# A decoder layer's first FFN group: gate and up blocks in one pass instead of two

## The chip, the cores and the metric

The kernel runs on one core of a Trainium2 chip. The metric is the device time of one execution in microseconds, from the host's point of view the time of the one launch; the profiled span, from the first to the last instruction of the program, is a little shorter. TensorE multiplies, ACT (ScalarE) and DVE (VectorE) work on the operands and results, SP (SyncE) and ACT issue the transfers from memory.

## The reference

A decoder layer on x of 256 rows and 2048 columns, float32: a half-weighted SwiGLU FFN, then a mixing stage (causal pooling, forgetting attention, memory cross-attention, gated and merged), then a second half FFN. The FFN is

```
def swiglu_half_ffn(x, norm_g, w_gate_up, w_down):
    h = rmsnorm(x, norm_g)
    gate, up = jnp.split(h @ w_gate_up, 2, axis=-1)
    return 0.5 * ((jax.nn.silu(gate) * up) @ w_down)
```

with w_gate_up of 2048 x 11264 (5632 gate columns, then 5632 up columns) and w_down of 5632 x 2048. This case is about the first 512 columns of gate and of up in the first FFN, the first thing that the kernel computes.

## The kernel before

**Products.** Every float32 operand is split in two parts, a high one that ACT writes (a copy in fp32r) and a low one that DVE writes (operand minus high). A product of 128 rows of weights by 512 columns is three matmuls: high by high, and the two mixed ones (add_product, lines 240 to 244; mm_group has its own loop, line 352). With 256 rows of x there are two row tiles t, so a k-tile (128 rows of weights) by a block (512 columns) takes six matmuls. A block has 16 k-tiles. Cutting weights into high and low is called a cut here; its tiles are wh and wl, five buffers each, 1024 columns wide.

**x.** The rows of x stay in four tiles xc of 512 columns each. `prepare(c, jj)` makes one page of the left side (tile names x, lines 200, 189, 190): four transposes on TensorE into a bank, then for each of two k-tiles a high part on ACT and a low part on DVE, both scaled by the norm's gains (`cols0`, made from a small load, a transpose and a copy, line 125). The row statistics are taken later (`row_sums`, eight squares on ACT, line 364; `row_rstd`, a chain of small steps on DVE from line 368 to 179) and are needed only by the gates, `gated`, lines 453 and 455. `row_sums` is pinned on ACT behind the ACT instruction that was traced just before it.

**Groups.** The FFN's 11 groups c each take 512 gate columns and 512 up columns. Groups 1 to 10 use `pair_group`: eight units of two k-tiles, each loaded as one raw tile (three buffers of 1 MB) with both blocks. For a unit listed in `seven`, the 2 x 2 blocks (two k-tiles, two blocks, two row tiles) are multiplied with seven block products instead of eight, that is 21 matmuls instead of 24. That needs a form page of x for the unit, made by `form_page` and kept in `forms`; which units are so treated is read at the call:

```
        seven = list(forms) if seven is None else seven
```

Form pages are made for the k-tile pairs 0, 1 and 2. The products of such a unit read the tiles hah, hal, hbh, hbl. A group with such units holds eight PSUM banks, one without holds four; there are eight in all. Group 0 does not use pair_group but two passes of `mm_group`: first the gate block over all 16 k-tiles, then the up block. In the first pass its loads are of 1, 1, 1, 1, 2, 2, 4 and 4 k-tiles, and the loads of x are placed between them by `before`.

**Order.** A planner orders each engine's instructions by the order in which they are traced and by its own times; `keep_in_program_order` pins an instruction behind the one traced before it on its engine. Work beside the products stands in the queue `side`; each `tick()` takes one entry from it. mm_group ticks after each cut; pair_group ticks after each block of a unit, for units that lie after the last unit with seven products, or for all when there is none. Before, the queue at the start holds a pause, `prepare(0, 1)`, a pause, the six other prepares, row_sums, three form pages, `small_loads`, three pauses and `small_cols`. `small_loads` issues eleven small loads on ACT's queue (tile rows); having no inputs, they may be issued early.

Of the kernel before, what the change touches and what calls it, by code (L numbers as in the profile page):

```python
# [16 lines left out]
P = 128  # L17
# [16 lines left out]
def hybrid_layer(  # L34
# [68 lines left out]
    def load_x(c0, n):  # L103
        tc.keep_in_program_order(
            nc.sync.dma_start(out=xc[c0 // 512][:, :, c0 % 512 : c0 % 512 + n], in_=xv[:, :, c0 : c0 + n])
        )
# [138 lines left out]
                ps, sides[part], wt[i][:, col : col + 512], start=start and q == 0, stop=stop and q == 2  # L245
            )

    def pair_group(w, c0, c1, lhs, forms, order, seven=None, hook=None, early=False):

        seven = list(forms) if seven is None else seven
        at = [i for i, u in enumerate(order) if u in seven]
        acc, terms = {}, {}

        def into(key, last):
            if key not in acc:
                acc[key] = bank("mm")  # L260
                return acc[key], True, last
            return acc[key], False, last

        for i, u in enumerate(order):
            end = i == len(order) - 1
            if hook:
                hook(i, u)
            raw = wp.tile([P, 2, 2, 512], F32, tag="raw", name="raw")
            for n, cc in enumerate((c0, c1)):
                nc.sync.dma_start(  # L270
                    out=raw[:, n, :, :],
                    in_=w[2 * u * P : (2 * u + 2) * P, cc : cc + 512].rearrange("(k p) c -> p k c", p=P),
                )
            if u not in seven:
                for n in range(2):
                    wt = parts(1024)
                    cut(wt, raw[:, n, :, :].rearrange("p k c -> p (k c)"))
                    for t in range(T):
                        for kk in range(2):
                            ps, start, stop = into((t, n), end and kk == 1)  # L280
                            add_product(ps, [lhs(2 * u + kk, q, t) for q in range(2)], wt, kk * 512, start, stop)
                    if not at or i > at[-1] or 1 < i < at[0] or (early and i == 0):
                        tick()
                continue
            last = i == at[-1]
            s = raw.rearrange("p n k c -> p (n k) c")
            plain = parts(1024)
            cut(plain, s[:, 0:2, :].rearrange("p s c -> p (s c)"))
            ta, tb = page([2, 512], F32, "ta"), page([2, 512], F32, "tb")
            nc.vector.tensor_tensor(ta, s[:, 3:4, :].to_broadcast([P, 2, 512]), s[:, 1:3, :], ALU.add)  # L290
            ha = (page([1024], F32R, "hah"), page([1024], F32R, "hal"))
            cut(ha, ta.rearrange("p s c -> p (s c)"))
            plain2 = parts(512)
            cut(plain2, s[:, 2, :])
            nc.vector.tensor_tensor(tb[:, 0, :], ta[:, 0, :], s[:, 2, :], ALU.add)
            nc.vector.tensor_tensor(tb[:, 1, :], tb[:, 0, :], s[:, 0, :], ALU.add)  # L296
            hb = (page([1024], F32R, "hbh"), page([1024], F32R, "hbl"))
            cut(hb, tb.rearrange("p s c -> p (s c)"))
            fm = lambda m: [forms[u][:, q, m, :] for q in range(2)]
            xq = lambda kk, t: [lhs(2 * u + kk, q, t) for q in range(2)]  # L300
            for key, sides, wt, col in (
                ("p1", xq(1, 0), plain, 512),
                ((0, 0), xq(0, 0), plain, 0),
                ("p5", fm(0), ha, 0),
                ("p7", fm(2), ha, 512),
                ((0, 1), fm(3), plain2, 0),
                ("p6", fm(1), hb, 0),
                ((1, 0), xq(0, 1), hb, 512),
            ):
                ps, start, stop = into(key, last if isinstance(key, str) else end)  # L310
                add_product(ps, sides, wt, col, start, stop)
            if last:
                a, u3, u4, v = (temp([512], n) for n in ("ua", "u3", "u4", "uv"))
                nc.scalar.activation(a, acc["p1"], AF.Copy)
                nc.vector.tensor_tensor(u3, acc["p6"], a, ALU.add)
                nc.vector.tensor_tensor(u4, acc["p5"], u3, ALU.subtract)
                nc.vector.tensor_tensor(u3, acc["p7"], u3, ALU.add)
                nc.vector.tensor_tensor(v, acc["p5"], u3, ALU.subtract)
                terms = {(0, 0): a, (1, 0): u3, (0, 1): u4, (1, 1): v}
        return acc, terms  # L320

    def mm_group(w, c0, kt, lhs, cols=((0, 512),), before=None):

        ncol = sum(n for _, n in cols)
        per, half = 2048 // ncol, 1024 // ncol
        ps = [[bank("mm") for _ in cols] for _ in range(T)]
        cuts = [0, 1, 2, 3, 4, 6, *range(8, kt + 1, per)] if before else [*range(0, kt, per), kt]
        for k0, k1 in zip(cuts, cuts[1:]):
            nk = k1 - k0
            if k0 % per == 0:  # L330
                whole = wp.tile([P, per, ncol], F32, tag="raw", name="raw")
            raw = whole[:, k0 % per : k0 % per + nk, :]
            load = nc.sync.dma_start(
                out=raw,
                in_=w[k0 * P : (k0 + nk) * P, c0 : c0 + ncol].rearrange("(k p) c -> p k c", p=P),
            )
            if before:
                tc.keep_in_program_order(load)
            if before:
                before(k0)  # L340
            for h0 in range(0, nk, half):
                nh = min(half, nk - h0)
                wh, wl = (b.rearrange("p (k c) -> p k c", c=ncol) for b in parts(half * ncol))
                rv, hv, lv = raw[:, h0 : h0 + nh, :], wh[:, :nh, :], wl[:, :nh, :]
                nc.scalar.activation(hv, rv, AF.Copy)  # L345
                nc.vector.tensor_tensor(lv, rv, hv.bitcast(F32), ALU.subtract)  # L346
                for t in range(T):
                    for kk in range(nh):
                        k = k0 + h0 + kk
                        for i, (o, n) in enumerate(cols):  # L350
                            for q, (part, wt) in enumerate(((0, wh), (0, wl), (1, wh))):
                                nc.tensor.matmul(  # L352
                                    ps[t][i][:, :n],
                                    lhs(k, part, t),
                                    wt[:, kk, o : o + n],
                                    start=k == 0 and q == 0,
                                    stop=k == kt - 1 and q == 2,
                                )
                tick()
        return ps  # L360
# [51 lines left out]
    def ffn(lx, forms, rs, wgu, wd, stream, cb, before=None):  # L412
# [34 lines left out]
        def gated(c, gate, up):  # L447
            hd = []
            for t in range(T):
                s = gate[t]  # L450
                if c == 0:
                    s = temp([512], "sg")
                nc.scalar.activation(s, gate[t], AF.Silu, scale=rs[0][:, t : t + 1])
                h = temp([512], "hd") if c == 0 else up[t]
                nc.vector.scalar_tensor_tensor(h, up[t], rh[:, t : t + 1], s, ALU.mult, ALU.mult)
                hd.append(h)
            return hd

        pa = mm_group(wgu, 0, KD, lx, before=before)
        nc.vector.tensor_scalar(rh, rs[0], 0.5, None, ALU.mult)  # L460
        pb = mm_group(wgu, FF, KD, lx)
        hd = gated(0, [pa[t][0] for t in range(T)], [pb[t][0] for t in range(T)])
        side.extend(put(0, hd))
        for c in range(1, NFC):
            if c == NFC - 1:
# [54 lines left out]
    def prepare(c, jj):  # L520
        to_lhs_part(tiles0, jj, lambda t: xc[c][:, t, :], G_FFN1[:, 4 * c : 4 * c + 4], "x0")

    def before(k0):

        if k0 == 0:
            prepare(0, 0)
        elif k0 == 1:
            load_x(256, 256)
        elif k0 == 3:
            load_x(512, 512)  # L530
        elif k0 == 6:
            load_x(1024, 512)
        elif k0 == 8:
            load_x(1536, 512)

    def row_sums(cs):
        for c in cs:
            for t in range(T):
                tc.keep_in_program_order(sumsq(ss0, t, c, xc[c][:, t, :]))

    side.extend(pause + [lambda: prepare(0, 1)] + pause)
    for c in range(1, 4):
        side.append(lambda c=c: prepare(c, 0))
        side.append(lambda c=c: prepare(c, 1))
    side.append(lambda: row_sums(range(4)) or rs0.append(row_rstd(ss0, "x0")))
    forms0 = {}
    side.extend(form_steps(forms0, tiles0))
    side.append(small_loads)
    side.extend(pause * 3 + [small_cols])
    s0 = Stream([xv[:, :, c * 512 : (c + 1) * 512] for c in range(4)])  # L550
    cb, x1, rs, s1 = residual(s0, G_MIX, "x1")
# [419 lines left out]
```

## Time and profile before

| | us |
|---|---|
| time, median of 3 runs (2128.15 to 2128.83) | 2128.67 |
| time of the profiled execution | 2128.03 |
| its span | 2126.3 |

TensorE's busy time is 99% of the span, DVE's 82%, ACT's 56%; the granted clock of TensorE is 1.00 throughout. A busy time counts a matmul from its start to its modelled end, and neighbours overlap; distances between starts tell more.

### The profile page before, as it was taken

Reading aid. Unit: us, or ns where it says so; the run is one execution under the profiler, and the core shown is the slowest. Engines: PE = TensorE matmul, PEld = TensorE weight load, DVE = VectorE, ACT = ScalarE, POOL = GpSimd, SP = SyncE. Lnnn points to the kernel's source line nnn. Section 1 sums busy time; section 2 is a strip of 40 time slices with the busy share of each in tenths; the row PEclk is TensorE's granted clock in tenths of the full one; section 3 lists DMA queues with packets and bytes.
Section 4 is the critical chain, followed back from the end, with each engine's and each line's share of the span. In section 5 each row is a group of like instructions: output and inputs, shape, how many; then the busy total and the mean of one; then the engine's idle time right before and its main releaser. Section 6 shows DMA issues by size and latency. Waiting matters only on the chain.

```text
span 2126.3 us, 26105 instructions
## 1 busy us (share of the span) xinstructions
PE 2114.2 (99%) x9683; PEld 1744.7 (82%) x9683; DVE 1739.4 (82%) x2221; ACT 1186.1 (56%) x1488; POOL 3.5 (0%) x24
## 2 busy tenths in 40 slices
PE   9999999999999999999999999999999999999999
PEld 7888888888888888887788888878888888888887
DVE  7898899889858788657669878898899889989675
ACT  6555555556545565555655555565555555556453
POOL 0000000000000000000000000000000000000000
PEclk9999999999999999999999999999999999999999
DMA  7666666666866654754456656575666666677764
GB/s 260 206 213 212 207 210 216 211 230 223 274 211 205 225 204 149 250 165 157 139 178 217 198 189 211 195 250 199 214 217 207 209 208 218 208 235 245 258 193 148
DMA packets 221508, 444.67 MB, mean 209 GB/s; under 512 B 12654, under 2 KB 13764, under 8 KB 221380
## 3 DMA queue, kind: packets, MB, share of 16 engines
q1 hardware_dynamic: 221088, 442.96, 62.7%
q8 instruction: 76, 1.25, 0.2%
q14 instruction: 52, 0.43, 0.1%
q10 hardware_dynamic: 292, 0.05, 0.0%
HBM read 426.16 MB, written 16.79 MB: 208 GB/s over the span
## 4 chain that ended last, share of the span: by engine, by line
PE 97%; DVE 1%; DMA 1%; ACT 0%; issue 0%; SPq 0%; ACTq 0%; DVEq 0%
PE mm L244 74%; PE mm L352 20%; PE hid L428 1%; DMA raw<-in_ffn_w_gate_up_dram 1%; DVE wl L346 0%; PE x L200 0%; DVE xr L389 0%; PE fpt L851 0%; PE fav L861 0%; PE mg L200 0%; PE flg L823 0%; PE mlg L729 0%; PE mav L756 0%; PE flg L821 0%; ACT wh L345 0%
## 5 line engine op out<-in xcount | busy, mean ns | idle before, releaser
L238 ACT ACTIVATE wh<-raw 128x1024 fp32r<-128x1024 f32 x608 | 599.7, 988 | 634.6 <-PE mm L244 362.5
L239 DVE TENSOR_TENSOR wl<-raw,wh 128x1024 fp32r<-128x1024 f32 x608 | 682.4, 1132 | 204.6 <-ACT wh L238 203.8
L244 PE MATMUL mm<-wh,x 128*128 128x512 f32 x2300 | 713.5, 391 | 0.0
L244 PEld LDWEIGHTS mm<-wh,x 128*128 128x128 f32 x2300 | 428.7, 188 | 87.3
L244 PE MATMUL mm<-wl,x 128*128 128x512 f32 x1150 | 446.7, 390 | 0.0
L244 PE MATMUL mm<-wh,hid 128*128 128x512 f32 x1168 | 357.7, 390 | 0.0
L352 PE MATMUL mm<-wh,x 128*128 128x512 f32 (+1 forms) x960 | 291.7, 382 | 2.9 <-ACT x L189 2.8
L346 DVE TENSOR_TENSOR wl<-raw,wh 128x1024 fp32r<-128x1024 f32 (+2 forms) x170 | 196.8, 1161 | 95.8 <-ACT wh L345 94.9
L345 ACT ACTIVATE wh<-raw 128x1024 fp32r<-128x1024 f32 (+2 forms) x170 | 170.5, 1009 | 169.7 <-PE mm L352 97.3
L244 PEld LDWEIGHTS mm<-wh,hid 128*128 128x128 f32 x1168 | 218.8, 188 | 45.1
L244 PEld LDWEIGHTS mm<-wl,x 128*128 128x128 f32 x1150 | 215.9, 188 | 45.3
L244 PE MATMUL mm<-wl,hid 128*128 128x512 f32 x584 | 222.4, 389 | 0.0
L352 PEld LDWEIGHTS mm<-wh,x 128*128 128x128 f32 x960 | 175.6, 188 | 38.6 <-ACT x L189 4.2
L352 PE MATMUL mm<-wl,x 128*128 128x512 f32 (+1 forms) x480 | 181.4, 379 | 0.2 <-DVE wl L346 0.2
L290 DVE TENSOR_TENSOR ta<-raw 128x1024 f32<-128x1024 f32 x101 | 123.1, 1219 | 12.0 <-DMA raw<-in_ffn_w_gate_up_dram 6.4
L244 PEld LDWEIGHTS mm<-wl,hid 128*128 128x128 f32 x584 | 109.6, 188 | 22.8
L239 DVE TENSOR_TENSOR hbl<-tb,hbh 128x1024 fp32r<-128x1024 f32 x101 | 123.2, 1220 | 2.5 <-ACT hbh L238 2.3
L239 DVE TENSOR_TENSOR hal<-ta,hah 128x1024 fp32r<-128x1024 f32 x101 | 123.2, 1220 | 1.4 <-ACT hah L238 1.4
L238 ACT ACTIVATE hbh<-tb 128x1024 fp32r<-128x1024 f32 x101 | 106.3, 1053 | 30.1 <-DVE tb L296 30.0
L238 ACT ACTIVATE hah<-ta 128x1024 fp32r<-128x1024 f32 x101 | 106.3, 1052 | 27.5 <-DVE ta L290 27.1
L244 PE MATMUL mm<-hah,form 128*128 128x512 f32 x404 | 121.5, 389 | 0.0
L352 PEld LDWEIGHTS mm<-wl,x 128*128 128x128 f32 x480 | 90.1, 188 | 16.3 <-DVE wl L346 0.6
(318 smaller groups left out, 2198.2 us busy)
## 6 DMA issues: line engine op xcount, KB each, us to landing
raw<-in_ffn_w_gate_up_dram SPq DMA_DIRECT2D x322, 512.0 KB, 4.5
raw<-in_ffn_w_down_dram SPq DMA_DIRECT2D x176, 512.0 KB, 5.1
raw<-in_w_in_dram SPq DMA_DIRECT2D x80, 512.0 KB, 5.1
raw<-in_w_in_dram SPq DMA_DIRECT2D x36, 1024.0 KB, 5.0
raw<-in_w_out_dram SPq DMA_DIRECT2D x32, 512.0 KB, 5.1
raw<-in_ffn_w_gate_up_dram SPq DMA_DIRECT2D x14, 1024.0 KB, 5.6
hd<-hf SPq DMA_DIRECT2D x20, 512.0 KB, 5.1
hg<-hd SPq DMA_DIRECT2D x20, 512.0 KB, 8.5
```

Source lines behind the costliest of these rows:

```text
L238: nc.scalar.activation(dst[0], src, AF.Copy)
L239: nc.vector.tensor_tensor(dst[1], src, dst[0].bitcast(F32), ALU.subtract)
L244: nc.tensor.matmul(ps, sides[part], wt[i][:, col : col + 512], start=start and q == 0, stop=stop and q == 2)
L290: nc.vector.tensor_tensor(ta, s[:, 3:4, :].to_broadcast([P, 2, 512]), s[:, 1:3, :], ALU.add)
L345: nc.scalar.activation(hv, rv, AF.Copy)
L346: nc.vector.tensor_tensor(lv, rv, hv.bitcast(F32), ALU.subtract)
L352: nc.tensor.matmul(ps[t][i][:, :n], lhs(k, part, t), wt[:, kk, o : o + n], start=k == 0 and q == 0, stop=k == kt - 1 and q == 2,)
L428: nc.tensor.transpose(ps[:, j, t * P : (t + 1) * P], hd[t][:, k * P : (k + 1) * P], ident)
```

## The change

Group 0 of the first FFN (the call with `before`) is now one pair_group over units 0 to 7 with both blocks, with no seven-product units, with `hook=before` and `pieces=2`. In a group with pieces every load on SP is pinned to the traced order. The first two units are loaded in four pieces, one for each k-tile and block, and cut piece by piece, 512 columns at a time; the others are loaded as two halves of 512 KB. `before` is now called with the unit's place: it loads x 256 to 511 and then 512 to 1023 ahead of unit 1, x 1024 to 1535 ahead of unit 3 and 1536 to 2047 ahead of unit 5, and it makes the pages of x for the following products. The queue now begins with `small_loads`, followed by 13 pauses, row_sums, the form pages, three pauses and small_cols.

```diff
-    def pair_group(w, c0, c1, lhs, forms, order, seven=None, hook=None, early=False):
+    def pair_group(w, c0, c1, lhs, forms, order, seven=None, hook=None, early=False, pieces=0):
...
-            for n, cc in enumerate((c0, c1)):
-                nc.sync.dma_start(
-                    out=raw[:, n, :, :],
-                    in_=w[2 * u * P : (2 * u + 2) * P, cc : cc + 512].rearrange("(k p) c -> p k c", p=P),
-                )
+            step = 1 if i < pieces else 2
+            for k in range(0, 2, step):
+                for n, cc in enumerate((c0, c1)):
+                    one = nc.sync.dma_start(
+                        out=raw[:, n, k : k + step, :],
+                        in_=w[(2 * u + k) * P : (2 * u + k + step) * P, cc : cc + 512].rearrange(
+                            "(k p) c -> p k c", p=P
+                        ),
+                    )
+                    if pieces:
+                        tc.keep_in_program_order(one)
+            if i < pieces:
+                for kk in range(2):
+                    for n in range(2):
+                        wt = parts(512)
+                        cut(wt, raw[:, n, kk, :])
+                        for t in range(T):
+                            ps, start, stop = into((t, n), False)
+                            add_product(ps, [lhs(2 * u + kk, q, t) for q in range(2)], wt, 0, start, stop)
+                    tick()
+                continue
...
-        pa = mm_group(wgu, 0, KD, lx, before=before)
-        nc.vector.tensor_scalar(rh, rs[0], 0.5, None, ALU.mult)
-        pb = mm_group(wgu, FF, KD, lx)
-        hd = gated(0, [pa[t][0] for t in range(T)], [pb[t][0] for t in range(T)])
+        if before:
+            ps, _ = pair_group(wgu, 0, FF, lx, {}, range(8), hook=before, pieces=2)
+            nc.vector.tensor_scalar(rh, rs[0], 0.5, None, ALU.mult)
+            up = [ps[t, 1] for t in range(T)]
+            hd = gated(0, [ps[t, 0] for t in range(T)], up)
+        else:
+            pa = mm_group(wgu, 0, KD, lx)
...
-    def before(k0):
+    def before(i, u):
-        if k0 == 0:
+        if i == 0:
             prepare(0, 0)
-        elif k0 == 1:
+        if i == 1:
             load_x(256, 256)
-        elif k0 == 3:
+            prepare(0, 1)
             load_x(512, 512)
-        elif k0 == 6:
+        if i == 2:
+            prepare(1, 0)
+        if i == 3:
             load_x(1024, 512)
-        elif k0 == 8:
+            prepare(1, 1)
+        if i == 4:
+            prepare(2, 0)
+        if i == 5:
             load_x(1536, 512)
+            prepare(2, 1)
+        if i > 5:
+            prepare(3, i - 6)
...
-    side.extend(pause + [lambda: prepare(0, 1)] + pause)
-    for c in range(1, 4):
-        side.append(lambda c=c: prepare(c, 0))
-        side.append(lambda c=c: prepare(c, 1))
+    side.extend(pause * 13)
     side.append(lambda: row_sums(range(4)) or rs0.append(row_rstd(ss0, "x0")))
     forms0 = {}
+    side.appendleft(small_loads)
     side.extend(form_steps(forms0, tiles0))
-    side.append(small_loads)
     side.extend(pause * 3 + [small_cols])
```

## Rows read from the trace of the kernel before

**Rows 1.** The page: its head, the busy time and share of each engine, and from the costliest groups the matmuls of weight sums with form pages (count, then busy us and mean ns).
```profile
span 2126.3 us, 26105 instructions
...
PE 2114.2 (99%) x9683; PEld 1744.7 (82%) x9683; DVE 1739.4 (82%) x2221; ACT 1186.1 (56%) x1488; POOL 3.5 (0%) x24
...
L244 PE MATMUL mm<-hah,form 128*128 128x512 f32 x404 | 121.5, 389 | 0.0
```

**Rows 2.** Busy time of each engine in three stretches: from and to, length, then busy us and count of PE, PEld, DVE, ACT and POOL, granted clock, share of the DMA engines, GB/s.
```profile
7.09:25.00 17.91, 16.39 (x82) 12.78 (x83) 11.73 (x19) 10.89 (x19) 0.00 (x0) 1.00 0.91 321
...
57.00:800.00 743.00, 743.00 (x3346) 615.17 (x3345) 626.68 (x739) 420.52 (x498) 0.00 (x0) 1.00 0.65 218
800.00:830.00 30.00, 27.97 (x135) 22.71 (x134) 27.20 (x61) 19.16 (x36) 0.00 (x0) 1.00 0.47 160
```

**Rows 3.** TensorE's waits, the whole span: who waited for whom, us in total, times, longest.
```profile
PE mm L352 <- ACT x L189: 2.8, 2, 1.4
```

**Rows 4.** The chain of work that ended last, of the first 75 or 30 us, in order of time: start, us, what.
```profile
5.69 2.37 DMA rows<-in_pool_scale_dram
...
8.08 0.38 SPq L105
...
8.50 5.73 DMA raw<-in_ffn_w_gate_up_dram
...
14.26 1.06 ACT wh L345
...
15.35 1.24 DVE wl L346
...
19.02 0.87 PE x L200 x8
...
24.41 10.89 PE mm L352 x48
```

**Rows 5.** TensorE alone in three stretches of the start: from and to, length, busy us and count of matmuls and transposes, granted clock, DMA share, GB/s.
```profile
7.09:13.33 6.24, 6.24 (x28) 1.00 0.64 198
13.33:15.72 2.39, 1.04 (x9) 1.00 1.06 386
15.72:18.85 3.13, 2.96 (x10) 1.00 1.05 390
```

**Rows 6.** SP's waits before it issues, first 26 us: us in total, times, longest.
```profile
SPq L105 <- DMA rows<-in_pool_scale_dram: 2.8, 1, 2.8
SPq L333 <- DMA rows<-in_fox_k_norm_dram: 1.1, 1, 1.1
```

**Rows 7.** Stretches of 1 us, columns as in rows 2.
```profile
5.00:6.00 1.00, 0.66 (x5) 0.42 (x4) 0.38 (x1) 0.90 (x2) 0.00 (x0) 1.00 1.05 374
...
9.00:10.00 1.00, 1.00 (x5) 0.76 (x5) 1.00 (x3) 0.53 (x2) 0.00 (x0) 1.00 0.71 172
...
11.00:12.00 1.00, 1.00 (x6) 0.81 (x6) 0.28 (x1) 0.00 (x0) 0.00 (x0) 1.00 0.86 257
...
20.00:21.00 1.00, 1.00 (x6) 0.83 (x5) 0.92 (x2) 0.88 (x3) 0.00 (x0) 1.00 1.04 385
```

**Rows 8.** The timeline of ACT: start, us, what, count, and the idle time before with its releaser.
```profile
4.96 1.36 ACT L345 ACTIVATE wh<-raw 128x512 fp32r<-128x512 f32 x2 [2.18 <-DMA raw<-in_ffn_w_gate_up_dram]
5.69 0.49 ACTq L148 DMA_DIRECT2D rows<-in_pool_scale_dram  x1
...
15.98 1.06 ACT L345 ACTIVATE wh<-raw 128x1024 fp32r<-128x1024 f32 x1 [0.30 <-DMA raw<-in_ffn_w_gate_up_dram]
```

**Rows 9.** The timeline of DVE at the start.
```profile
5.62 0.69 DVE L346 TENSOR_TENSOR wl<-raw,wh 128x512 fp32r<-128x512 f32 x1 [3.29 <-ACT wh L345]
6.23 0.17 DVE L125 COPY cols<-pcols 128x16 f32<-128x16 f32 x1
...
7.07 0.48 DVE L190 SCALAR_TENSOR_TENSOR x<-x,cols,x 128x256 fp32r<-128x256 f32 x1
```

**Rows 10.** Groups of TensorE's instructions from 56.8 to 99.3 us, which is group 1: those with the weight sums hah.
```profile
L244 PE MATMUL mm<-hah,form 128*128 128x512 f32 x12 | 3.7, 389 | 0.0
```

**Rows 11.** The timeline of TensorE in group 1: its first matmul, and the first one with form pages in two units with seven products.
```profile
56.88 0.62 PE L244 MATMUL mm<-wh,x 128*128 128x512 f32 x2
...
63.68 0.62 PE L244 MATMUL mm<-hah,form 128*128 128x512 f32 x2
...
73.88 0.62 PE L244 MATMUL mm<-hah,form 128*128 128x512 f32 x2
```

**Rows 12.** The timeline of ACT: the first and the last of the eight squares of the row sums.
```profile
27.87 0.62 ACT L364 ACTIVATE junk<-xc 128x512 f32<-128x512 f32 x1
...
32.16 0.62 ACT L364 ACTIVATE junk<-xc 128x512 f32<-128x512 f32 x1
```

**Rows 13.** The timeline of DVE: the first and the last step of the row statistics, and the last product of group 0's gates.
```profile
33.15 0.15 DVE L368 TENSOR_REDUCE x0r<-ss 128x2 f32<-128x8 f32 x1
...
46.55 0.17 DVE L460 TENSOR_SCALAR rh<-x0y 128x2 f32<-128x2 f32 x1
...
58.65 0.74 DVE L455 SCALAR_TENSOR_TENSOR hd<-mm,rh,sg 128x512 f32<-128x512 f32 x1
```

**Rows 14.** DMA issues of the first 75 us by size: count, KB each, median us from issue to landing.
```profile
raw<-in_ffn_w_gate_up_dram SPq DMA_DIRECT2D x18, 512.0 KB, 5.3
...
raw<-in_ffn_w_gate_up_dram SPq DMA_DIRECT2D x4, 256.0 KB, 3.4
```

More of the change, by code (lines that the diff above doesn't have):

```diff
@@ L457, in gated @@
             return hd
-        pa = mm_group(wgu, 0, KD, lx, before=before)
-        nc.vector.tensor_scalar(rh, rs[0], 0.5, None, ALU.mult)
-        pb = mm_group(wgu, FF, KD, lx)
-        hd = gated(0, [pa[t][0] for t in range(T)], [pb[t][0] for t in range(T)])
+        if before:
[5 more added lines that the diff above has]
+            pa = mm_group(wgu, 0, KD, lx)
+            nc.vector.tensor_scalar(rh, rs[0], 0.5, None, ALU.mult)
+            pb = mm_group(wgu, FF, KD, lx)
+            hd = gated(0, [pa[t][0] for t in range(T)], [pb[t][0] for t in range(T)])
         side.extend(put(0, hd))
```

## Prediction

> **What bounds the kernel now.** I began with the head of the page: TensorE is busy for 2114.2 of the 2126.3 us span, so everything that can be won without removing matmuls lies in 12.1 us of idle time and in slots that a "busy" TensorE wastes [rows 1]. Next, the windows by stage: from 57 to 800 us TensorE has no idle time at all, at granted clock 1.00, so nothing that another engine does there can show; it is idle in the first 25 us, and for 2 us near 807 [rows 2]. The waits of TensorE name what it lacked at the start: split x, 2.8 us in two waits [rows 3].
>
> A matmul's own duration is no price, since matmuls overlap. The price is the distance from one start to the next, read from the chain where TensorE never waits: 48 in 10.89 us, 0.227 each; eight transposes took 0.87, so 0.109 each [rows 4]. With these I measured what the first group loses after its first matmul at 7.09 us [rows 5]:
> - 7.09 to 13.33 us holds 24 matmuls (the k-tiles 0 to 3 of the gate) and 4 transposes: 5.45 + 0.44 = 5.89 of 6.24, lost 0.35.
> - 13.33 to 15.72 holds eight transposes, 0.87 of 2.39: lost 1.52.
> - 15.72 to 18.85 holds 10 matmuls, 2.27 of 3.13: lost 0.86.
>
> Together 2.73 us; from there on the starts stand close. The chain says why: the weights of k-tiles 4 and 5 were issued at 8.50 behind the x load of 8.08, which waited 2.8 us on SP for a small row load of ACT's queue (pool_scale, issued 5.69, over at 8.06); they landed at 14.24, then came a cut of 1.06 on ACT and one of 1.24 on DVE [rows 4, 6]. In the meantime little flowed: 172 GB/s from 9 to 10 us against 385 later [rows 7]. So the start is bound by when weights land, and 2.73 us is all that this stage has to give after 7.09.
>
> **The change, part by part.**
>
> *Gate and up together.* The same 192 matmuls, 32 transposes and bytes; the order differs. The first 24 matmuls now need k-tiles 0 and 1 of both blocks (1 MB, as four k-tiles of gate did) but only half as much x: the loads on SP are x 0 to 255, four pieces of 256 KB, x 256 to 511, x 512 to 1023, four more pieces. By place in that order the seventh load is the 512 KB of x, just as now. I take it to be issued at 8.08 again, since the same small loads come from ACT. Then what TensorE lacks after its first 24 matmuls is the first piece of unit 1 (256 KB) and no longer a 512 KB load. The rows: 512 KB landed at 14.24, and the next 512 KB let ACT begin at 15.98, so 256 KB takes about 0.85 and the piece is there near 13.4 [rows 4, 8]. Its cut of 512 columns takes 0.68 on ACT (1.36 for two) instead of 1.06, and 0.69 on DVE instead of 1.24 [rows 4, 8, 9]. Its first matmul comes at about 14.1.
>
> TensorE gets there at 7.09 + 5.89 + 0.5 = 13.48. The 0.5 is the present 0.35 plus a little: the new order uses low x as its second matmul, not its third, and low x is written from 7.07 to 7.55 [rows 9]. So it waits 0.6, or less if the transposes of x 512 to 1023 are put there; I take 0.4. The third matmul waits for the low part, another 0.2. After that each piece lasts 1.36 us on TensorE (6 matmuls), longer than a piece's load of 0.85 and than its cuts: no further stall. New loss 0.5 + 0.4 + 0.2 = 1.1, gain 2.73 - 1.1 = 1.6. Bounds: all of 2.73 if nothing waits; from below, a loss of 0.6 if the pieces come at the slow rate of 9 to 12 us (rival 2).
>
> *x in smaller doses.* No transposed page is late in the new order: x 1024 on is needed only at unit 4, three units of 24 x 0.227 = 5.45 us after unit 1 began. Cost nothing.
>
> *Smaller cuts and more DMAs.* Eight 512-wide cuts and twelve 1024-wide instead of four and fourteen: +0.2 us on ACT, +0.3 on DVE, hidden by TensorE's saturation (DVE 82%, ACT 56% of the span) [rows 1]. Eight more loads (20 instead of 12) delay only SP, which from unit 3 on waits for free buffers.
>
> *The hidden part: ticks.* The side queue advances once per tick. The old two passes give 10 + 8 = 18, enough for the three form pages. The new group gives 2 in each of units 0 and 1 and 2 in each of the other six: 16. The queue now is small_loads, 13 pauses, row_sums, form page 0: that is 16. Pages 1 and 2 are not made when group 1 is called, and `seven = list(forms)` is read there, once. So group 1 has one unit with seven products instead of three (now 12 hah matmuls, four per such unit) [rows 10]. A unit of seven costs 21 matmuls, a plain one 24; the starts of two seven-units with one plain unit between them stand 10.20 apart, 45 x 0.227 [rows 11]. Two units lose 6 matmuls: +1.36 us. Nothing hides this; TensorE is saturated there. The transposition of the small columns moves into group 1 at the same price.
>
> *Sums and gates.* The row sums are pinned on ACT behind the cut of unit 7's gate block. Five wh buffers allow that cut once TensorE is through unit 4's up block, near 38 us (14.1 + 5.45 for unit 1, three units more, 16 transposes at 0.109). The eight squares take 4.9 us (27.87 to 32.8 now) and the chain on DVE from the reduction to rh took 13.4 [rows 12, 13]: rs between 46 (14 steps of some 0.17, one right behind the other) and 58, while group 0 ends near 55. Group 1 first needs a fifth bank after 24 matmuls, 5.45 us later, at 60.4. Hidden, with 2 us to spare in the slow case; without that cover each us late is a us lost.
>
> *Small pieces as such.* From 5 to 6 us, with loads of 256 KB in flight, the rate was 374 GB/s, against 385 for the 1 MB loads at 20 [rows 7]; one of 256 KB landed in 3.4 us, one of 512 KB in 5.3 [rows 14]. So several small pieces in flight cost nothing in the sum. A rule speaks against the change here: the Trainium skill, "DMA: Bandwidth & Descriptors", section "Measured (HBM→SBUF, 128 partitions, SWDGE, issued from GpSimd)", says to batch DMAs to at least 1 MiB, below which the rate falls; its table is for another way of issuing, which no run here uses. By that rule the gain of 1.6 would shrink to about nothing and the sum would end near +1.4; the 374 speaks against it.
>
> **Sum.** -1.6 + 1.36 = -0.25 us. The profiled execution took 2128.03 (span plus 1.73); 2127.8 by it. The runs' median is 2128.67, 0.64 above it, so 2128.4.
>
> **The rivals.**
> 1. *The start becomes smooth.* The x load finds an earlier turn and no piece is late: -2.73 + 1.36 = -1.4, 2127.3. For it: SP issued nothing for the 2.8 us before 8.08 [rows 6]. Against: the same small loads of ACT are still there.
> 2. *The pieces come slowly*, because SP waits for small loads between them as it does before the x load. At about 215 GB/s, the middle of the 172 to 257 of 9 to 12 us, instead of 385 [rows 7], unit 1's 1 MB takes 4.9 us instead of 2.7: 2.2 us come back, of which the 0.6 that I had as stalls at that place can be the same time. The gain is then 1.6 - 2.2 + 0.6 = 0, net +1.4, 2130.1; without that overlap 0.6 more. For it: SP waited for another small load too, fox_k, 1.1 us [rows 6]. Against: 374 GB/s with small loads about. The page cited above would expect the same from the size alone.
> 3. *The banks of group 0 are freed late* (the slower side). Group 0 now holds four banks to its end; group 1's first seven-unit needs four more. If rs comes more than about 5 us after the end of group 0, TensorE stalls one for one; at 9.3 us after it (a chain on DVE of some 20 us instead of 13.4) the loss passes 4.3 us, 2133. For it: row sums come later than today. Against: the chain's steps are short, and the gates' last product is done by 59.4, 2.5 us after group 0 [rows 13].
> 4. *The first matmul moves.* Today x waits for cols, copied at 6.23 behind a low cut that began at 5.62 [rows 9]; put first, it saves up to 0.6, and two small loads put ahead of x on ACT (0.49 each [rows 8]) cost up to 1: 2127.8 to 2129.4.
>
> **How the numbers follow.** Forecast 0.5, rival 1 0.17, rival 2 0.2, rival 3 0.05, rival 4 0.08. A measurement of this kernel can tell some 0.2% from no change, 4.3 us. Forecast and rivals 1, 2 and 4 all lie within it; faster needs more than the 2.73 us that exist (0.02); slower is rival 3 at its far end, or a new order far downstream that opens a wait like the 2 us near 807 several times over (0.05). Same: 0.93. The range runs from rival 1 with the 0.6 of an earlier x and 0.3 for differences between runs, 2126.4, to rival 2 with its 0.6 and 0.4, 2131.1.
>
> **What would show it.** Right: hah,form x396 on the page instead of 404 [rows 1] and six more matmuls in group 1; group 1 starts near 55 instead of 56.88 [rows 11]; PE's waits for split x shrink from 2.8 to about 2; pool_scale still ahead of the x load. Wrong, if hah stays at 404 (ticks miscounted, 1.4 us faster), if the 512 KB of x is issued well before 8, or if TensorE waits between 58 and 66 us.

## The result: 5 us slower, and the profile after

The changed kernel took 2133.76 us, median of 9 runs (2132.56 to 2136.52), the kernel before 2128.67 us beside it (9 runs): ratio 1.0025, 95% interval 1.0016 to 1.0033. The forecast of 2128.4 and its range to 2131.1 were too low; "slower" had been given 0.05. The profiled execution of after took 2132.56 us, its span is 2130.8 us against 2126.3 [rows 1].

The page of after: its head, the busy times, and from the groups by form the matmuls of weight sums with form pages, which answer to [rows 1].

```profile
span 2130.8 us, 26131 instructions
...
PE 2117.3 (99%) x9689; PEld 1747.6 (82%) x9689; DVE 1732.6 (81%) x2213; ACT 1182.3 (55%) x1486; POOL 3.5 (0%) x24
...
L244 PE MATMUL mm<-hah,form 128*128 128x512 f32 x396 | 119.0, 389 | 0.0
```

Six matmuls more and 396 instead of 404: the two lost seven-product units are there as forecast. By the prediction's price they cost 1.36 us (measured for itself among the experiments). The waits of TensorE, to be held against [rows 3] (us in total, times, longest), show the rest:

```profile
PE mm L244 <- ACT x L189: 4.5, 3, 3.1
```

It waits for split x as before, but 4.5 us instead of 2.8, and one wait alone is 3.1 us. The timeline of TensorE says where. These rows answer to [rows 11]; the last one is group 1's first matmul.

```profile
7.30 2.07 PE L244 MATMUL mm<-wh,x 128*128 128x512 f32 x4 [0.89 <-ACT x L189]
...
38.20 1.36 PE L200 MATMUL x<-ident,xc 128*128 128x128 f32 x11
42.70 1.43 PE L244 MATMUL mm<-wh,x 128*128 128x512 f32 x5 [3.14 <-ACT x L189]
...
46.13 1.42 PE L244 MATMUL mm<-wh,x 128*128 128x512 f32 x5 [0.43 <-ACT x L189]
...
59.86 0.61 PE L244 MATMUL mm<-wh,x 128*128 128x512 f32 x2
```

Group 1 begins at 59.86, not at 56.88 as before and not near 55 as forecast. At 38.20 TensorE makes eleven of the twelve transposes for the pages of units 5, 6 and 7 one behind the other and then stands for 3.14 us until the first of these pages is split; it stands again before unit 6. What ACT did meanwhile is on its timeline, against [rows 12]:

```profile
38.16 1.06 ACT L238 ACTIVATE wh<-raw 128x1024 fp32r<-128x1024 f32 x1 [1.61 <-PE mm L244]
39.13 0.61 ACT L380 ACTIVATE junk<-xc 128x512 f32<-128x512 f32 x1
...
41.58 0.61 ACT L380 ACTIVATE junk<-xc 128x512 f32<-128x512 f32 x1
42.10 0.19 ACT L380 ACTIVATION_READ_ACCUMULATOR junk<-xc 128x1 f32 x1
42.19 0.45 ACT L189 ACTIVATE x<-x,cols 128x256 fp32r<-128x256 f32 x1
...
45.10 0.62 ACT L226 ACTIVATE form<-ff 128x512 fp32r<-128x512 f32 x1
45.62 0.46 ACT L189 ACTIVATE x<-x,cols 128x256 fp32r<-128x256 f32 x1
```

The cut of unit 7's gate block ran at 38.16, and the pinned squares followed it at once: five of the eight stand ahead of the high part of unit 5's page (42.19), the rest and a form page ahead of unit 6's (45.62). Five squares of 0.61 us are 3.06 us, the length of the wait.

In the kernel before the same squares ran from 27.87 on [rows 12], behind the last high parts of pages (timeline of ACT), and TensorE had no idle time from 25 to 57 us (window, columns as in [rows 2]):

```profile
25.21 0.87 ACT L189 ACTIVATE x<-x,cols 128x256 fp32r<-128x256 f32 x2 [0.28 <-DVE x L190]
```

```profile
25.00:57.00 32.00, 32.00 (x142) 26.21 (x141) 29.72 (x57) 23.92 (x39) 0.00 (x0) 1.00 0.70 236
```

The ledger of both pairs of profiled executions (the second one of each kernel is among the experiments; these two ran on different chips) uses the prediction's prices, 0.2267 us for a matmul and 0.1088 for a transpose; what the distance between two starts has beyond that is lost:

| us | forecast | first pair | second pair |
|---|---|---|---|
| first matmul: before, after | no change | 7.09, 7.30: +0.21 | 7.32, 7.31: -0.01 |
| lost from it to 25 us | 2.73 to 1.1: -1.6 | 2.79 to 1.75: -1.04 | 2.53 to 0.51: -2.02 |
| lost from 25 us to group 1 | 0 | 0.31 to 4.23: +3.92 | 0.31 to 5.12: +4.81 |
| two units of 24 for 21 | +1.36 | +1.36 | +1.36 |
| sum | -0.25 | +4.45 | +4.14 |
| difference of the spans | | +4.5 | +4.9 |

The first, second and fourth line came as forecast or nearly (the fourth is the price, not a reading); the third was put at nothing. The ledger leaves out two things. The transposition of the small columns moved from group 0 into group 1: from group 1's first product to group 2's the traces have 42.43 us in both executions of before and 44.23 and 44.22 in those of after, so 0.4 more than the 1.36. And what lies behind group 1 differs between executions of one kernel: 2026.99 and 2026.04 us in the two of before.

### The profile page after: what moved, and what is told of

Same layout as the page of the kernel before. It is cut to its first block, busy times and chain, and to the rows that moved or that the text cites. A ratio compares the mean times of both kernels' runs of the same rounds, so it can differ in the third digit from the quotient of the medians.

```text
span 2130.8 us, 26131 instructions
## 1 busy us (share of the span) xinstructions
PE 2117.3 (99%) x9689; PEld 1747.6 (82%) x9689; DVE 1732.6 (81%) x2213; ACT 1182.3 (55%) x1486; POOL 3.5 (0%) x24
## 4 chain that ended last, share of the span: by engine, by line
PE 97%; DVE 1%; ACT 0%; issue 0%; DVEq 0%; ACTq 0%
PE mm L244 75%; PE mm L368 18%; PE hid L444 1%; PE x L200 0%; PE fpt L878 0%; DVE wl L362 0%; DVE xr L405 0%; PE fav L888 0%; PE mg L200 0%; PE flg L850 0%; PE mlg L756 0%; PE mav L783 0%; PE flg L848 0%; PE fav L890 0%; PE fav L889 0%
## 5 line engine op out<-in xcount | busy, mean ns | idle before, releaser
L238 ACT ACTIVATE wh<-raw 128x1024 fp32r<-128x1024 f32 (+1 forms) x628 | 617.9, 986 | 652.4 <-PE mm L244 365.8
L239 DVE TENSOR_TENSOR wl<-raw,wh 128x1024 fp32r<-128x1024 f32 (+1 forms) x628 | 703.1, 1129 | 224.2 <-ACT wh L238 222.1
L244 PE MATMUL mm<-wh,x 128*128 128x512 f32 x2452 | 760.4, 392 | 4.5 <-ACT x L189 4.5
L244 PE MATMUL mm<-wl,x 128*128 128x512 f32 x1226 | 474.8, 390 | 0.0
L368 PE MATMUL mm<-wh,x 128*128 128x512 f32 (+1 forms) x832 | 251.2, 380 | 0.1
L362 DVE TENSOR_TENSOR wl<-raw,wh 128x1024 fp32r<-128x1024 f32 (+1 forms) x152 | 177.2, 1167 | 88.4 <-ACT wh L361 87.7
L361 ACT ACTIVATE wh<-raw 128x1024 fp32r<-128x1024 f32 (+1 forms) x152 | 153.8, 1015 | 159.2 <-PE mm L368 94.5
L368 PE MATMUL mm<-wl,x 128*128 128x512 f32 (+1 forms) x416 | 156.3, 376 | 0.0
L368 PEld LDWEIGHTS mm<-wl,x 128*128 128x128 f32 x416 | 78.2, 188 | 13.4 <-issue 0.3
```

Source lines behind the costliest of these rows:

```text
L238: nc.scalar.activation(dst[0], src, AF.Copy)
L239: nc.vector.tensor_tensor(dst[1], src, dst[0].bitcast(F32), ALU.subtract)
L244: nc.tensor.matmul(ps, sides[part], wt[i][:, col : col + 512], start=start and q == 0, stop=stop and q == 2)
L368: nc.tensor.matmul(ps[t][i][:, :n], lhs(k, part, t), wt[:, kk, o : o + n], start=k == 0 and q == 0, stop=k == kt - 1 and q == 2,)
```

## The experiments

The theory: the wait at 39 us is made by the squares that stand on ACT ahead of unit 5's page, so it goes when the order on ACT changes, whatever work is done. Against it stood the lost units, the pages themselves (made right before they are used), the squares' work as such on a full ACT, and a start that had grown slower.

All ratios are to runs of the kernel before on the same chip.

**Squares not pinned.** The planner may put them where ACT has time.

```
-                tc.keep_in_program_order(sumsq(ss0, t, c, xc[c][:, t, :]))
+                sumsq(ss0, t, c, xc[c][:, t, :])
```

> The changed kernel with one edit: the eight squares of the row sums are no longer pinned on ACT behind the cut of unit 7's gate block. Theory A (the squares stand ahead of the split of unit 5's x page on ACT): the planner can now put them where ACT is idle, so TensorE's waits of 3.3 us at 39.3 and 0.6 at 45.3 go: 2133.8 - 3.9 = 2129.9, within 0.5 of it; hah stays at 396. Theory B (that page is simply made late, its transposes start only at 38.2): a wait of at least 1 us stays at unit 5, 2131 to 2133. Theory C (the slow TensorE before 10.5 us makes the loss): no change, 2133.8.

Measured: 2128.76 us (11 runs; before 2128.2), ratio 1.0002, interval 0.9993 to 1.0011. The timeline of ACT around the same place, then that of TensorE:

```profile
37.09 1.06 ACT L238 ACTIVATE wh<-raw 128x1024 fp32r<-128x1024 f32 x1 [1.61 <-PE mm L244]
38.06 1.19 ACT L189 ACTIVATE x<-x,cols 128x256 fp32r<-128x256 f32 x3
```

```profile
37.13 1.25 PE L200 MATMUL x<-ident,xc 128*128 128x128 f32 x10
38.57 1.79 PE L244 MATMUL mm<-wh,x 128*128 128x512 f32 x5 [0.19 <-ACT x L189]
...
55.41 0.62 PE L244 MATMUL mm<-wh,x 128*128 128x512 f32 x2
```

The squares now ran earlier, in pairs, between 10.2 and 28.7 us. The page follows the cut directly, the wait is 0.19 us, and from 25 us to group 1 0.91 us are lost instead of 4.23. Group 1 begins at 55.41, where the prediction had it. By the two ratios this one edit gives back 0.0023, 4.9 us; the slowdown is gone. That is more than theory A's 3.9, and 2128.76 lies below its 2129.4 to 2130.4; 0.5 us of this is that the kernel before was faster on this chip too. What is left of the change is, within the interval, the -0.25 us of the prediction's sum.

**Form pages earlier.** They stand at the ninth to eleventh tick, so that all three are there when group 1 is called; the row sums keep their tick and their pin.

```
-    side.extend(pause * 13)
-    side.append(lambda: row_sums(range(4)) or rs0.append(row_rstd(ss0, "x0")))
-    side.appendleft(small_loads)
-    side.extend(form_steps(forms0, tiles0))
+    side.append(small_loads)
+    side.extend(pause * 7)
+    side.extend(form_steps(forms0, tiles0))
+    side.extend(pause * 3)
+    side.append(lambda: row_sums(range(4)) or rs0.append(row_rstd(ss0, "x0")))
```

> The changed kernel with one edit: the three form pages are taken from the queue at ticks 9 to 11, before the row sums, which keep tick 15. All three pages then exist when group 1 is called: hah 404 again, six matmuls fewer, -1.4 us: 2132.4 if the ticks are counted rightly and nothing else moves; 2133.8 if the lost units cost nothing. The wait at unit 5 stays under A and B, by A a little shorter if fewer squares stand ahead.

Measured: 2130.86 us (11 runs), ratio 1.0014, interval 1.0004 to 1.0023. The product count falls back by six, to 9683, but the wait stays, now before unit 5 and before unit 6 (timeline of TensorE):

```profile
40.71 1.45 PE L244 MATMUL mm<-wh,x 128*128 128x512 f32 x5 [2.63 <-ACT x L189]
...
44.76 1.45 PE L244 MATMUL mm<-wh,x 128*128 128x512 f32 x5 [1.00 <-ACT x L189]
```

Four squares ran ahead of the page here instead of five, and the first wait is 2.63 instead of 3.14. 4.33 us are lost from 25 us to group 1, as in after. So the lost units are a term of their own, and the wait does not come from them. By the ratios this edit gives back 0.0011, 2.3 us, against 1.4 expected; the intervals allow both.

**Both repairs together.**

> Both edits, squares unpinned and form pages early. Theory A with the lost units: 2133.8 - 3.9 - 1.4 = 2128.5, about the kernel before. Theory B: 2130 or more. Theory C: 2132.4 or more.

Measured: 2126.43 us (11 runs), ratio 0.9992, interval 0.9983 to 1.0000; on another chip the same kernel took 2126.57 us, ratio 0.9990, interval 0.9981 to 0.9999. The windows up to group 1 (columns as in [rows 2]):

```profile
7.33:25.00 17.67, 17.65 (x86) 14.36 (x87) 15.34 (x32) 11.91 (x25) 0.00 (x0) 1.00 0.89 316
25.00:57.00 32.00, 32.00 (x147) 26.42 (x146) 27.56 (x46) 23.53 (x37) 0.00 (x0) 1.00 0.75 258
```

Against 16.39 busy of 17.91 us before [rows 2] TensorE is all but without a gap from its first product on; group 1 begins at 54.57. This is the change as the diff would have it, without its two side effects: some 2 us faster than before (2128.2 - 2126.43 = 1.8; 2128.15 - 2126.57 = 1.6), of the 2.73 that the prediction found there to win. One interval ends at 1.0000 and the other at 0.9999, so the gain is at the edge of what can be told from no change. The 2128.5 expected from theory A was 2 us too high.

> The kernel with both repairs, without the filling matmul: some 2 us below before, as it was on the other chip (ratio 0.9992). In this profile too no wait of TensorE for split x longer than 0.3 us between 25 and 62 us.

That second execution shows the same: 0.14 us lost from 25 us to group 1, which begins at 54.30.

**Pages earlier, squares still pinned.** The last load of x and the pages of units 5 to 7 come one or two units earlier.

```
         if i == 4:
             prepare(2, 0)
+            prepare(2, 1)
+            load_x(1536, 512)
         if i == 5:
-            load_x(1536, 512)
-            prepare(2, 1)
-        if i > 5:
-            prepare(3, i - 6)
+            prepare(3, 0)
+            prepare(3, 1)
```

> The changed kernel with one edit: the x pages of units 5, 6 and 7 are traced a unit or more earlier (units 5's with 4's, 6's and 7's with 5's), the last x load with unit 4; the squares stay pinned. Theories A and B both say that unit 5's wait goes, since its page is then split before the squares: about -3.5 us, 2130.3. If the squares themselves delayed the cuts, a wait for weights would show near 45 us instead and the time would stay above 2132.

Measured: 2131.0 us (11 runs), ratio 1.0013, interval 1.0005 to 1.0022: better than after, no repair. The timelines of TensorE and of ACT:

```profile
32.54 1.36 PE L200 MATMUL x<-ident,xc 128*128 128x128 f32 x11
35.92 1.20 PE L244 MATMUL mm<-wh,x 128*128 128x512 f32 x4 [2.02 <-ACT wh L238]
```

```profile
33.06 0.47 ACT L189 ACTIVATE x<-x,cols 128x256 fp32r<-128x256 f32 x1 [6.28 <-PE x L200]
34.09 0.84 ACT L189 ACTIVATE x<-x,cols 128x256 fp32r<-128x256 f32 x2 [0.55 <-DVE x L190]
34.82 1.05 ACT L238 ACTIVATE wh<-raw 128x1024 fp32r<-128x1024 f32 x1
...
43.93 0.61 ACT L380 ACTIVATE junk<-xc 128x512 f32<-128x512 f32 x1
...
48.22 0.61 ACT L380 ACTIVATE junk<-xc 128x512 f32<-128x512 f32 x1
```

Two things are seen. The eight squares now run in one block from 43.93 to 48.83, with no page behind them, and TensorE loses nothing from 38 us to group 1: the same pinned squares are free where nothing that TensorE waits for stands behind them. And the same fault has come up elsewhere: ACT stood idle for 6.28 us with the page's high part at the head of its order, waiting for transposes that TensorE made only at 32.54, while the cut of unit 4's weights stood behind it (in after the same cut ran at 23.92); TensorE then waited 2.02 us for that cut. The wait names wh this time, not x; the cause is again what stands ahead on ACT.

The Trainium skill, "TensorE: Matmul & The Clock Gate", section "Architectural detail: the array is 16× 32×32, not 1× 128×128", says that ACT's queue is strictly first in, first out. These rows agree: 6.28 idle us with a cut behind.

**Every square twice.** More work on ACT at the same pinned place.

```
-                tc.keep_in_program_order(sumsq(ss0, t, c, xc[c][:, t, :]))
+                for _ in range(2):
+                    tc.keep_in_program_order(sumsq(ss0, t, c, xc[c][:, t, :]))
```

> The changed kernel with each of the eight pinned squares done twice: ACT gets 4.9 us more of the same work at the same place, behind the cut of unit 7's gate block. The planner, with more squares to place, traces out with one square ahead of the high part of unit 5's page instead of five. Theory (what stands ahead of the page on ACT sets the stall): TensorE's wait at 39 us shrinks from 3.1 us to about 0.7, and the later pages meet two to four squares each, so the time falls by 2 to 3 us below the changed kernel, to about 2131, though ACT has more to do. Rival (the squares' work itself, ACT being full there): 3 to 5 us slower than the changed kernel, 2137 or more.

Measured: 2128.58 us (10 runs; before 2127.91), ratio 1.0004, interval 0.9995 to 1.0013. With 4.9 us more work on ACT it is 0.0021 faster than after, 4.5 us. The timelines of ACT and of TensorE:

```profile
38.07 1.06 ACT L238 ACTIVATE wh<-raw 128x1024 fp32r<-128x1024 f32 x1 [1.61 <-PE mm L244]
39.03 0.61 ACT L380 ACTIVATE junk<-xc 128x512 f32<-128x512 f32 x1
...
39.65 1.18 ACT L189 ACTIVATE x<-x,cols 128x256 fp32r<-128x256 f32 x3
```

```profile
38.11 1.36 PE L200 MATMUL x<-ident,xc 128*128 128x128 f32 x11
40.15 1.43 PE L244 MATMUL mm<-wh,x 128*128 128x512 f32 x5 [0.68 <-ACT x L189]
```

Up to 39.03 the two kernels run alike. Then one square stands ahead of the page instead of five, and TensorE waits 0.68 us instead of 3.14: the difference of 2.46 is four squares (4 x 0.61 = 2.44). The experiments together show the wait growing with the number of squares ahead of the page: 0.19 us with none, 0.68 with one, 2.63 with four, 3.14 with five. The amount of work on ACT is no cause; the order is.

By the ratios the gain is larger than the 2 to 3 us expected: the second wait is gone too (1.06 lost from 25 us to group 1, 3.2 less than in after's first profile, 4.1 less than in its second, below). The two profiled spans differ by 2.4 only, 2130.8 and 2128.4, as what lies behind group 1 took 0.8 more here.

**The price of two seven-product units alone.** The kernel before with one form page ahead of group 1 and two behind the small columns.

```
-    side.extend(form_steps(forms0, tiles0))
+    side.extend(form_steps(forms0, tiles0, 1))
     side.append(small_loads)
-    side.extend(pause * 3 + [small_cols])
+    side.extend(pause * 5 + [small_cols])
+    side.extend(form_steps(forms0, tiles0)[1:])
```

> The kernel before, with only form page 0 made ahead of group 1; pages 1 and 2 are made behind the small columns, so that group 1 has one unit with seven products instead of three, as in the changed kernel. Theory: two units of 24 instead of 21 matmuls, six matmuls of 0.227 us in a stage without idle time, cost 1.36 us: some 1.2 to 1.6 us above before. Rival (the seven-product units win less than their matmuls, since TensorE's work on the form pages and DVE's extra sums take it back): within 0.5 us of before.

Measured: 2129.57 us (11 runs; before 2127.91), ratio 1.0008, interval 0.9999 to 1.0017, that is +1.7 us (-0.2 to +3.6). It has the same x396 and 9689 products as after. The interval alone would also allow the rival's 0.5; the traces do not. Here group 1's first product starts at 56.49 and group 2's at 100.29, 43.79 us later; in both profiles of before it is 42.43 (56.88 to 99.31 in the first). The difference is 1.36.

**A second profiled execution of both kernels.**

> The kernel before, unchanged, for a second profiled execution. If the half pace of the first products is a matter of the order of the new first group, the starts after the first product stand 227 ns apart here as they did in the first profile. If it comes and goes by execution, this profile may show it too: starts 427 ns apart for some microseconds after 7.1 us.

> The changed kernel, unchanged, for a second profiled execution. The wait at 39 us is a matter of ACT's order, which is fixed in the program, so it shows again at 3.0 to 3.3 us. The first products' spacing may be 427 ns or 227 ns, as it differed between the two profiles of the kernel before.

Before: 2127.03 us; after: 2131.96 us (one run each, on two chips). The first products of before started 427 ns apart this time, those of after 227 ns apart: it is the other way round than in the first profiles. So the half pace belongs to the execution, not to the order of the first group. The wait at 39 us came again as it had to, 3.13 us, but with something behind it (timeline of TensorE, then the windows with the granted clock ahead of the DMA share):

```profile
36.93 1.36 PE L200 MATMUL x<-ident,xc 128*128 128x128 f32 x11
41.43 1.43 PE L244 MATMUL mm<-wh,x 128*128 128x512 f32 x5 [3.13 <-ACT x L189]
42.70 0.59 PE L244 MATMUL mm<-wl,x 128*128 128x512 f32 x1
43.09 0.63 PE L244 MATMUL mm<-wh,x 128*128 128x512 f32 x1
43.51 0.63 PE L244 MATMUL mm<-wl,x 128*128 128x512 f32 x1
...
47.04 0.39 PE L244 MATMUL mm<-wl,x 128*128 128x512 f32 x1
```

```profile
42.00:43.00 1.00, 1.00 (x5) 0.86 (x4) 1.00 (x2) 1.00 (x3) 0.00 (x0) 0.86 0.00 0
43.00:44.00 1.00, 1.00 (x4) 0.72 (x3) 0.84 (x4) 1.00 (x5) 0.00 (x0) 0.50 0.00 0
```

After the wait the granted clock fell to 0.50, the lower level of 1.2 GHz, and stayed there to 46 us; seven starts stand 427 ns apart (7 x 0.2 = 1.4 us lost). The second wait, for unit 6's page, does not appear: at half pace TensorE came to it late enough. So the stop can cost more than its own length: from 25 us to group 1 5.12 us are lost here and 4.23 in the first profile.

**A filling matmul at the start.** One more warm-up matmul between the first transposes and the first product, on top of both repairs.

```
+            tc.keep_in_program_order(nc.tensor.matmul(pwarm, warm[:, :P], warm, start=True, stop=True))
```

> The kernel with both repairs (squares not pinned, form pages at earlier ticks) plus one more warm-up matmul in float32 between the first transposes and the first product, where TensorE otherwise stands idle from 5.7 to 7.1 us. Theory (the idle time just ahead of the first product lets TensorE start the products at the lower of its two levels, 427 ns from one start to the next instead of 227): with the gap filled, the starts of the first products stand 227 ns apart from the first on, and the time falls by 0.5 to 1.5 us below the kernel with both repairs. Rival (the half pace at the start comes and goes from one execution to the next, whatever the kernel does there): no difference of more than 0.5 us, and the half pace may be seen or not.

> The kernel with both repairs and the filling matmul, beside the same kernel without the filling (below) on one chip. Theory (the filling keeps the lower level away or ends it sooner): 0.5 to 1.5 us below the kernel without it, and its runs closer together. Rival (it only fills time in which nothing was wanted): the two within 0.4 us of each other.

Measured: 2125.04 us (11 runs; before 2127.91), ratio 0.9989, interval 0.9980 to 0.9998; beside the kernel without it on one chip 2126.11 against 2126.57, ratios 0.9990 for both. Neither profile with the filling shows products at half pace, but neither do the two without it (at most a start or two), so what it was to prevent was not there to be prevented. The 0.46 us between the two cannot be told from nothing; whether the filling keeps the half pace away stays open. With it the kernel is 2.9 and 2.0 us below before on the two chips.

## Why the prediction was wrong

**What bounds the kernel: right.** From the first product to 25 us there were 2.73 us to win, and with both repairs 0.5 are left lost there (2.79 before).

**Gate and up together: right that most of the loss goes, with a spread it had not counted.** Forecast: from 2.73 to 1.1 lost. Measured 1.75 and 0.51 in two executions of after. That their mean is 1.13 is luck: 0.6 of the 1.1 was to be a stall at the first piece of unit 1, and neither execution has one there (0.34 shows only with the squares unpinned, where the cut of that piece began at 13.83, right behind two of them). ACT's first piece of unit 1 was to be there near 13.4; the cut began at 13.50 (13.66 in the second execution, the one that lost less):

```profile
13.50 0.63 ACT L238 ACTIVATE wh<-raw 128x512 fp32r<-128x512 f32 x1 [1.54 <-DMA raw<-in_ffn_w_gate_up_dram]
```

The 512 KB of x were issued at 8.31, near the 8.08 forecast, but for another reason, so this was luck too. SP again waits 2.9 us ahead of that load (2.8 in [rows 6]), now for the load of x issued at 5.00 and no longer for pool_scale. The semaphore numbers in the traces say why: the load waits for the earlier transfer that signals on the semaphore it takes over, number 101 of pool_scale before and number 102 of that load of x, landed at 8.30, now.

What made the spread is the pace of the first products (last section), not the transfers: the half pace overlapped with the late weights in the kernel before, where it cost nothing (2.53 lost at half pace, 2.79 at full pace). In the new order it costs about 1 us: 1.72 to 1.80 are lost in the three profiles with half pace, 0.43 to 0.94 in the seven without.

**Ticks: right.** 396, and 1.36 us (measured in the kernel before with one seven-product unit).

**Small pieces: right.** No wait of TensorE for weights is left in the first 57 us of after; rival 2 did not come. By the prediction's own prices the smaller cuts cost ACT 4 x 0.68 - 2 x 1.06 = 0.6 us and not 0.2; nothing hangs on it.

**"x in smaller doses … Cost nothing" and "Sums and gates … Hidden": here it failed.** The second of these steps placed the pinned squares correctly, behind the cut of unit 7's gate block and near 38 us (38.16), and gave them 4.9 us of ACT. It then followed them only forwards, into the row statistics and the gates: those were in time indeed (rh at 54.66, no wait of TensorE from 50 to 62 us; rival 3 did not come):

```profile
54.66 0.17 DVE L477 TENSOR_SCALAR rh<-x0y 128x2 f32<-128x2 f32 x1
```

What it did not ask is what stands behind the squares on ACT itself. The first of the two steps looked at the pages only for whether x had been loaded, and it had been. But the diff makes each page right before the unit that uses it, by the hook, where the old queue had made it many ticks ahead (the last one was split from 25.21 on, before the squares began). A page made at the last moment has no time to spare, and pinned work put at the same moment on the engine that has to split it is paid in full until the page's turn comes: five of the eight squares, 3.1 us, and 3.9 to 4.8 us with what followed. The sum had 0 for this. Both facts were in the text, 38 us for the squares and "x 1024 on is needed only at unit 4" (14.1 + 5.45 and so on, so unit 5 at about 38); they were not laid beside each other.

**Faster, same, slower.** With that term at nothing the sum was -0.25, and the kernel with only the squares unpinned shows what it then would have been: ratio 1.0002. The slower side was reserved for rival 3 and "a new order far downstream"; the new wait was in the first group itself. None of the prediction's signs of being wrong appeared (no wait of TensorE between 58 and 66 us); three of its signs of being right failed: the start of group 1 near 55, the waits for split x near 2, and pool_scale ahead of the x load.

## What to carry to other kernels

When an edit moves work on an in-order engine, write down what stands behind it on that engine, who waits for each of these and how much time each has to spare; where the work's own result is needed is only half of the question. Operands that are made right before their use can turn a burst on the engine that makes them into a stop of TensorE; a pin, right in the old order, has to be looked at again when the order around it changes. And an idle engine is no sign of room: ACT stood for 6.28 us in one of these kernels with the work that mattered behind it.

## What the hardware showed beside it

The first products of some executions start 427 ns apart instead of 227, and the transposes ahead of them 213 instead of 109, for some 5 us (5.1 to 10.4 us in after's first profile). In after's first profile the granted clock reads 1.00 through that time; in the kernel with doubled squares, where the starts have the same 427 ns from 8 to 11 us, the record says 0.50 (windows, granted clock ahead of the DMA share; after's first, then those of the doubled squares):

```profile
8.00:9.00 1.00, 1.00 (x4) 0.78 (x3) 0.48 (x1) 0.27 (x1) 0.00 (x0) 1.00 0.00 1
```

```profile
8.00:9.00 1.00, 1.00 (x5) 0.70 (x4) 0.48 (x1) 0.16 (x2) 0.00 (x0) 0.50 0.00 1
...
11.00:12.00 1.00, 1.00 (x5) 0.83 (x4) 0.46 (x2) 0.47 (x1) 0.00 (x0) 0.86 0.90 229
```

By these distances after's TensorE too is at the lower of its two levels there, and a clock column of 1.00 at the very start of a profile is no proof of the upper one: the distances between starts are. The Trainium skill, "TensorE: Matmul & The Clock Gate", section "Part 1: The HAM clock gate (the "warmup" mystery)", gives 426.7 ns from start to start for 512 columns at the lower level and 215.7 at the upper, and says that how much of a start runs slow differs from run to run. The 427 agrees, as does the difference from run to run; at the upper level the rows here show 227, and the sums of this text use that.

The second thing is the fall after a wait of 3.13 us in the middle of the kernel, with 1.4 us of half pace behind it, in one execution of two with the same wait. The median of after lies 1.2 us above its first profiled execution, in which the fall did not happen. The mean granted clock on record for each execution points to such falls as the reason. Of after's nine, the five with a mean of 0.997 or 0.998 took 2133.70 to 2136.52 us, the four with 0.999 or 1.000 2132.56 to 2133.76. A mean of 0.998 or less stands beside 14 of the 31 executions of the three kernels in which TensorE stood for over 2 us (after, form pages earlier, pages earlier), beside 7 of the 76 of the other kernels tried, and beside 2 of the 81 of the kernel before run with them. Where in the span the clock was low is on record only for the profiled ones.
